# Four accumulator banks in a written order, and attention pieces spread over the key/value tile

## The chip, the cores and the metric

The kernel runs on one core of a Trainium2 chip. The metric is the device time of one execution in microseconds (us): the kernel before takes 1521.53 us, median of 3 runs (1521.13 to 1522.24).

## The reference

One layer of a hybrid decoder in float32, width 1024: a half-step SwiGLU feed-forward, a mixer, a second half-step feed-forward, each with RMS norms before and after. 512 prompt tokens with 16 meta tokens in front, and 8 running sequences with 4 new tokens each (32 sample tokens), go through the same weights. The mixer adds a gated linear attention (4 heads) and a stick-breaking attention (16 heads of 64). The latter is the part the change touches:

```
z = einsum('bqhd,bkhd->bhqk', q, k) * scale + bias
l = where(mask, log_sigmoid(-z), 0)
r = cumsum(l, reverse) - l
a = where(mask, exp(log_sigmoid(z) + r), 0)
o = einsum('bhqk,bkhd->bqhd', a, v)
```

The sample tokens attend in the same way over 256 cached positions, read by a page table, and their own.

## The kernel before

**Tiles.** Activations lie transposed, features on partitions and the 560 tokens (512 + 16 + 32) along the free axis, in two halves of 280. A weight is used as a high part (rounded by a cast) and a low part (weight minus high part, on VectorE); three products of parts make one full product. Large products go by a Strassen-like scheme: `seven_steps` forms seven products of quarter matrices in four accumulators a, d, b, c. Its groups, of 12 matmuls each, run in the order a, d, b, d (second, here d2), c, a, c; the second d group uses the quarter pair "b2", the b group uses "t", the sum of quarters. Before b's group, ScalarE copies a into b (`S.copy(b, a)`, L1059); likewise b into c. Copies such as "e5" (L1049) read d away.

**Attention pairs.** The heads go in eight pairs. In the steady part a pair is a query tile (8 steps on TensorE, `Pair.queries`, one product with two accumulators, one for each token half) and a key/value tile (14 steps, `values_keys`, by `seven_steps`). While the tiles of one pair run, the pieces of the attention of the pair before are dealt out: `scores` (a head's scores in three PSUM banks, two sigmoids on each bank, L1997 "keep" and L1998 "beta", causal masks on GpSimd, L2002), `scan` (running products on VectorE, L2011, in four pieces of 144, 272, 400 and 528 columns), `weigh` (one product of 1343 columns and two copies, L168 and L2022), `rows_v` and `rows_k` (transposes and outputs), `tails`, `turned` (transposes of the weights, L2073). The query tile ends in `queries`: ScalarE writes the high part (L1914), VectorE the residual (L171) and sample columns (L1923), both reading the query accumulators.

**Order.** Within the mixer the order of TensorE, VectorE, ScalarE and GpSimd is the order in which the program issues: a table of steps says behind which step of the tile a piece is issued (`pieces` in the list that `then` fills, and `weights_at` for the casts and low parts of the weight quarters b1, t, b2, t4). Each engine executes its own list in order, so an instruction that waits holds all behind it. SyncE issues most transfers in order; GpSimd issues the accumulating ones (L644, L649), which add a second weight block onto one that SyncE has loaded (L640, L641, L648).

**Banks.** Accumulators come from a pool of four PSUM buffers under one tag. A buffer is chosen when an accumulator is first written in program order: the one that has been free longest. In the key/value tile, a is written first, then b (by the copy, in issue order), then d, and d gets the buffer of the query tile's first half, last read by L171.

**Rooms.** SBUF is cut into rooms. Which one each `take` gets is written in a table, `PLACES`, made for one order of the program. Two uses of a room must not overlap, so a new user waits for the last reader.

**Samples.** From the fifth pair on, transposes of cached keys (`sample_keys`, L2176, at steps SK) and products with them (`sample_products`, L2190, at steps SP) are dealt in too; the pages are asked for a pair ahead (L2128).

Of the kernel before, what the change touches and what calls it, by code (L numbers as in the profile page):

```python
# [16 lines left out]
P = 128  # L17
# [36 lines left out]
1824065c540c372a763c3e20808c6e5292844e4a507a82727c62787464608e0288408670324c121e66947e583b2e10466844420122348a901400  # L54
5a126c30486a3f171456582a38003a040c8e3654026460147486324c5c401e94707e68884319106622268a34906a2428480842066c30844a9278
7a8c62520c2e5080402a6e1d1c7d181a084e825c5a3f100c120a7c207214461d092a2e42085c447d1a3f6e061b130c0f2b7c5a0a182c107d4647
5c086f1944410f16135e6e2c2a180c5a7c3f6f1a460d5d195b16410e121518142e446e2a7c6f5a0c1c1a410d5c15141146126e2c186f2a2b1c5a
7d0e0c4115145c467c0e2e6e6f7d2a2c1918415c1c145d6b7a7c0e100c746e62643284683a8e382a7888701876045224008c4836902e608a1c42
5c867e9270065e401a2a1218451d426a2e2c765a343f1c182d762a772f182b2c3f1b1c2a762f1b1c2e2b2c2d2a485a122a0626081b453a648c38
7072762924868a900c6e362e88000e04623f0a341c3230084e06418e7c6c281b60822484261e01733937110d687402922c2a422e21718d3b9189  # L60
6f6605878b65506a945453447851460f18585621807e41666019767c1a22508e6c6a1e525118202125416a84261e7468501842922e822c282a24
067a203f145a124a5e160a5c4c884172646e86056a034870398a903a92930c2e008c37113625822c026422527a3f343a5a501c140d7224869041
68200518848a926a2e261e6e6f9332742a302539061a03640a8c6872824c205c2c22528604127a368418904a5e320c378a1143426a2e39912888
25000418021a1c41172484924e8c682a707212506e30647a6f143f1634624a0c078a0d060a0811483c906874883e5e281e5f2a5a6a8c70422236
382c2e5052647a8272620c866e342549203c122c2a3a365c1e1f2e5a144a4c2f4812082a383406251f0a3c2a48122f5a32304a1e23165e215c06
3b08391f362c340a3c125a3625485e3032123b4d2a085c062c162e4a0a5e213428363c262b485a5e30321e2a25061428224d080a123c163f5c26
5e3634082b48123c5b363a483230381e4d4b2508285e260a16065c14224a383a5a482e2a08123c06374822341e2e2c2030363f2508483d4c4a3c
5a345c285f2620131e2a08155a373f251f060a322e2c0812303c3834363a481e3d4a15135f4c3208382a1e300a3c5a2512203806322c222b2e1e
0a4c085c5e364a3034483215063c083e22365a1234280232152026124a142a18406252309284242c50383a281e0a624c2e481032170008223e16
50483c200626405228141e343000241402062c9284402e62164c08521e223e160a3e0026244c002862480a20503c4c062c481614002e50183f52  # L70
1416081e0a4a222b12202a3d062d0a0800023c17411a4e2e1e1c16143f2a18040252223c2e1e414e080a2a002c20161206181c003e1a403c521e
2212142e5c842f3a324f16623834925a4e09362928245c07305e842e2a284f5b244c2c22485c201e28244e93925e5a295051245c849204504b48
4e294f240c5a648e46944282807c90726a8a667a707476887e446c55608c00683461380a32366f023c783a184f4e406216861b04143e126e1d1c
614e504a525854559248768e4d091b06023c7818601b843b7430643a60003236348d680a380b391b8c886e60446c687e6d8d557170668b8a6780
# [62 lines left out]
def hybrid_step(  # L137
# [17 lines left out]

    def whole(n):

        r = [take(3 * NT) for _ in range(-(-n // 3))]
        return [r[i // 3][:, NT * (i % 3) : NT * (i % 3) + NT] for i in range(n)], r

    count = [0]

    def ps(tag="ps"):
        count[0] += 1
        return pp.tile([P, 512], F32, tag=tag, name=f"{tag}{count[0]}")

    def tt(out, a, b, op, eng=None):
# [2614 lines left out]
```

## Time and profile before

| | |
|---|---|
| median of the runs | 1521.53 us |
| the profiled execution | 1521.29 us |
| its span | 1519.6 us |
| TensorE busy | 1486.7 us, 98% |
| VectorE busy | 1103.6 us, 73% |
| ScalarE busy | 820.7 us, 54% |
| GpSimd busy | 81.3 us, 5% |

The profiled execution lies inside the range of the timed runs; 1.7 us of it lie outside the span. The eight attention pairs take the stretch from about 570 to 830 us. Rows of the chip's timeline read: start, duration, engine, line, operation, output and input tiles, shape, count, and in brackets the idle time before it with what ended it. A row with "x4" covers four instructions from the first start to the last end.

### The profile page before, as it was taken

What the parts mean: (1) busy time and instruction counts of PE and PEld (TensorE: products, weight loads), DVE (VectorE), ACT (ScalarE), POOL (GpSimd) and SP (SyncE); (2) the same over time, 40 slices, a digit from 0 to 9 for tenths busy, and PEclk for the clock granted to TensorE, in tenths of its full rate; (3) what the DMA queues carried; (4) which work ended last, traced back from release to release, by engine and by line L of the source; (5) the groups of instructions that cost most, each with busy time, mean ns of one, the idle gap of its engine ahead of it and who ended that gap; (6) DMA issues with size and microseconds to landing.
All of it is one profiled execution on the core that took longest, in us unless ns stands there. A gap on an engine that the chain in (4) does not pass through costs nothing.

```text
span 1519.6 us, 29801 instructions
## 1 busy us (share of the span) xinstructions
PE 1486.7 (98%) x11825; PEld 1435.8 (94%) x11825; DVE 1103.6 (73%) x1860; ACT 820.7 (54%) x1537; POOL 81.3 (5%) x175
## 2 busy tenths in 40 slices
PE   9999999999999999899889999999999999999998
PEld 8999999999999888888778999999999999999998
DVE  5888888944677767777767745666567998888554
ACT  6545454633655647667665644644564554455434
POOL 2000000000000121112211000000000000000000
PEclk9999999999999999999999999999999999999999
DMA  8123333334673795556665766534632333332253
GB/s 248 56 84 99 97 98 98 89 99 142 163 155 108 177 167 134 99 112 117 136 94 148 218 162 215 114 97 107 180 109 80 93 99 98 111 98 86 86 153 113
DMA packets 288541, 187.61 MB, mean 123 GB/s; under 512 B 10988, under 2 KB 266674, under 8 KB 288402
## 3 DMA queue, kind: packets, MB, share of 16 engines
q1 hardware_dynamic: 280706, 181.97, 45.2%
q0 software_dynamic: 7680, 3.74, 2.5%
q8 instruction: 93, 1.52, 0.4%
q14 instruction: 46, 0.38, 0.1%
q10 hardware_dynamic: 16, 0.00, 0.0%
HBM read 160.63 MB, written 25.03 MB: 122 GB/s over the span
## 4 chain that ended last, share of the span: by engine, by line
PE 91%; DVE 4%; ACT 2%; issue 1%; DMA 1%; SPq 1%; DVEq 0%; ACTq 0%
PE acc L1291 8%; PE acc L1290 7%; PE acc L1289 7%; PE acc L732 6%; PE acc L733 6%; PE acc L735 6%; PE acc L719 5%; PE acc L720 4%; PE acc L722 4%; PE acc L1069 4%; PE acc L1071 4%; PE acc L1070 4%; PE acc L1232 2%; PE acc L1229 2%; PE acc L1230 2%; DVE room L168 1%
## 5 line engine op out<-in xcount | busy, mean ns | idle before, releaser
L168 DVE TENSOR_TENSOR room<-room,room 128x560 fp32r<-128x560 f32 (+17 forms) x451 | 290.4, 664 | 82.5 <-ACT room L799 18.3
L168 DVE TENSOR_TENSOR lo<-raw,hi 128x1024 fp32r<-128x1024 f32 (+1 forms) x207 | 248.0, 1199 | 95.7 <-ACT hi L697 48.4
L1291 PE MATMUL acc<-room,lo 128*128 128x280 f32 (+1 forms) x896 | 260.0, 290 | 0.0
L1290 PE MATMUL acc<-room,hi 128*128 128x280 f32 (+1 forms) x896 | 259.6, 290 | 0.0
L1289 PE MATMUL acc<-room,hi 128*128 128x280 f32 (+1 forms) x896 | 259.5, 290 | 0.0
L997 ACT CAST hi<-raw 128x1024 fp32r<-128x1024 f32 x114 | 120.1, 1057 | 142.7 <-PE acc L1290 49.3
L719 PE MATMUL acc<-room,hi 128*128 128x280 f32 x608 | 174.8, 304 | 0.2 <-DVE room L171 0.2
L1069 PE MATMUL acc<-room,hi 128*128 128x280 f32 x476 | 149.0, 313 | 23.8 <-DVE room L171 22.8
L1291 PEld LDWEIGHTS acc<-room,lo 128*128 128x128 f32 x896 | 168.8, 188 | 0.0
L1289 PEld LDWEIGHTS acc<-room,hi 128*128 128x128 f32 x896 | 168.7, 188 | 0.0
L1290 PEld LDWEIGHTS acc<-room,hi 128*128 128x128 f32 x896 | 168.5, 188 | 0.0
L720 PE MATMUL acc<-room,hi 128*128 128x280 f32 x608 | 163.9, 289 | 0.0
L1071 PE MATMUL acc<-room,lo 128*128 128x280 f32 (+1 forms) x476 | 141.4, 297 | 0.1
L1070 PE MATMUL acc<-room,hi 128*128 128x280 f32 (+1 forms) x476 | 141.0, 296 | 0.0
L697 ACT CAST hi<-raw 128x1024 fp32r<-128x1024 f32 (+1 forms) x93 | 93.6, 1006 | 76.2 <-issue 22.7
L997 ACT CAST hi<-room 128x1024 fp32r<-128x1024 f32 x106 | 89.4, 843 | 82.0 <-PE acc L1290 59.9
L168 DVE TENSOR_TENSOR lo<-room,hi 128x1024 fp32r<-128x1024 f32 x106 | 101.2, 955 | 44.0 <-ACT hi L997 43.8
L722 PE MATMUL acc<-room,lo 128*128 128x280 f32 x608 | 126.1, 289 | 0.0
L719 PEld LDWEIGHTS acc<-room,hi 128*128 128x128 f32 x608 | 114.4, 188 | 7.7 <-issue 5.6
L1069 PEld LDWEIGHTS acc<-room,hi 128*128 128x128 f32 x476 | 92.5, 194 | 30.4 <-issue 28.6
L720 PEld LDWEIGHTS acc<-room,hi 128*128 128x128 f32 x608 | 114.6, 189 | 0.9
L732 PE MATMUL acc<-room,hi 128*128 128x280 f32 (+2 forms) x388 | 110.7, 295 | 0.0
(405 smaller groups left out, 3654.0 us busy)
## 6 DMA issues: line engine op xcount, KB each, us to landing
raw<-in_w_in_dram SPq DMA_DIRECT2D x68, 256.0 KB, 5.1
raw<-in_ffn_w_gate_dram SPq DMA_DIRECT2D x64, 256.0 KB, 3.2
raw<-in_ffn_w_up_dram SPq DMA_DIRECT2D x64, 256.0 KB, 3.4
raw<-in_ffn_w_down_dram SPq DMA_DIRECT2D x36, 448.0 KB, 3.7
raw<-in_w_in_dram SPq DMA_DIRECT2D x29, 512.0 KB, 7.3
out_dram<-room SPq DMA_DIRECT2D x36, 256.0 KB, 5.4
room<-in_cache_k_dram SPq DMA_DIRECT2D x32, 256.0 KB, 5.5
room<-in_cache_v_dram SPq DMA_DIRECT2D x32, 256.0 KB, 5.8
```

Source lines behind the costliest of these rows:

```text
L168: (eng or V).tensor_tensor(out=out, in0=a, in1=b, op=op)
L719: T.matmul(acc[h][:, :w], hi[k], act.get(k, h, w)[0], start=(k == order[0]), stop=False, skip_group_check=True)
L720: T.matmul(acc[h][:, : wid[h]], hi[k], a[h][1], start=False, stop=False, skip_group_check=True)
L722: T.matmul(acc[h][:, : wid[h]], lo[k], a[h][0], start=False, stop=(k == order[-1]), skip_group_check=True)
L732: T.matmul(acc[h][:nw, : wid[h]], wh, a[h][0], start=(k == 0), stop=False)
L997: S.copy(hi[:, :kt], src)
L1069: T.matmul(x[:, :n], hi, act_[k][0][:, :n], start=(first and k == 0), stop=False, skip_group_check=True)
L1070: T.matmul(x[:, :w], hi, act_[k][1][:, :w], start=False, stop=False, skip_group_check=True)
L1071: T.matmul(x[:, :w], lo, act_[k][0][:, :w], start=False, stop=(k == 3), skip_group_check=True)
L1289: T.matmul(x[:, :QW], hi, act[k][0], start=(first and k == 0), stop=False, skip_group_check=True)
L1290: T.matmul(x[:, :QW], hi, act[k][1], start=False, stop=False, skip_group_check=True)
L1291: T.matmul(x[:, :QW], lo, act[k][0], start=False, stop=(k == 3), skip_group_check=True)
```

## The change

Four things are rewritten.

- **Banks.** The accumulators have four buffers of one tag each (acc0 to acc3), taken in a written rotation; `seven_steps` and the feed-forward's seven products each permute the rotation for those that follow. In the key/value tile of a plain pair d now takes the buffer that c had a pair earlier, last read by a ScalarE copy; b takes that of query half 0, c that of query half 1.
- **Scores by bank.** `scores` is called for one bank at a time, at steps 2, 3, 5 for the first head and 7, 10, 12 for the second, instead of all three at steps 2 and 4.
- **Pieces.** Scans, weightings, key rows and tails follow: the first weighting at step 9 instead of 7, the second at 14 instead of 12; key rows at 11 instead of 8. Steps 1 to 8 are the query tile, 9 to 22 the key/value tile. In the weight parts, t is cast one step sooner, b2 two steps later, t4 one. Sample keys, sample products and the page loads move too.
- **Rooms.** `PLACES` is a new table for the new order.

```diff
-1824065c540c372a763c3e20808c6e5292844e4a507a82727c62787464608e0288408670324c121e66947e583b2e10466844420122348a901400
+1824062b1f3c5a12107a7792469472788c90324c6a888286487e8e3a68804a0284406c7c643655448a30622f1666607050524e0c3874426e560c
...
+    pa = ctx.enter_context(tc.tile_pool(name="pa", bufs=1, space=bass.MemoryType.PSUM))
...
-    count = [0]
+    count, banks = [0], [0, 1, 2, 3]
 
     def ps(tag="ps"):
         count[0] += 1
+        if tag == "acc":
+            banks.append(banks.pop(0))
+            return pa.tile([P, 512], F32, tag=f"acc{banks[-1]}", name=f"acc{count[0]}")
         return pp.tile([P, 512], F32, tag=tag, name=f"{tag}{count[0]}")
...
-    def weights_at(when, n, f, sums=(-10, -10, -9, -8), b1=(-6, -5)):
+    def weights_at(when, n, f, sums=(-10, -10, -9, -8), b1=(-6, -5), t=(-2, -1), b2=(0, 1), t4=(4, 6)):
...
-        for key, d, e in (("b1", *b1), ("t", -2, -1), ("b2", 0, 1), ("t4", 4, 6)):
+        for key, d, e in (("b1", *b1), ("t", *t), ("b2", *b2), ("t4", *t4)):
...
         a, d, b, c = (ps("acc") for _ in range(4))
+        banks[:] = [banks[i] for i in (2, 1, 0, 3)]
...
             a, d, b, c = (ps("acc") for _ in range(4))
+            banks[:] = [banks[i] for i in (2, 0, 1, 3)]
...
-        def scores(self, e):
+        def scores(self, e, n):
...
-            for n, what in enumerate(BANKS):
...
+            if n == 0:
+                self.wide[e] = take(NW_), take(NW_)
+            beta, keep = self.wide[e]
+            at = (0, 416, 832)[n]
+            p = ps()
+            c = 0
+            for i, k0, k1 in BANKS[n]:
...
-            if e:
+            if e and n == 2:
                 give(*qs, *ks)
...
-    SK, SP, TURN = (7, 9, 11, 12), (11, 14), (15, 16, 17, 18, 19, 20)
+    SK, SP, TURN = (4, 7, 13, 14), (9, 16), (15, 16, 17, 18, 19, 20)
...
-                weights_at(then, BEGIN[pr] + TILE, ("kv", pr), (-6, -6, -5, -4))
+                weights_at(then, BEGIN[pr] + TILE, ("kv", pr), (-6, -6, -5, -4), t=(-3, -2), b2=(2, 3), t4=(5, 7))
...
-            pieces = [(2, now.scores, 0), (3, now.scan, 0, 0), (3, now.scan, 0, 1), (3, now.meta), (4, now.scores, 1), (4, now.scan, 0, 2),
-                      (5, now.scan, 0, 3), (6, now.rows_v), (7, now.weigh, 0), (8, now.rows_k), (9, now.scan, 1, 0), (9, now.scan, 1, 1),
-                      (10, now.scan, 1, 2), (10, now.tails), (11, now.scan, 1, 3), (12, now.weigh, 1)]
+            pieces = [(2, now.scores, 0, 0), (3, now.scores, 0, 1), (3, now.meta), (3, now.scan, 0, 0), (3, now.scan, 0, 1), (5, now.scores, 0, 2),
+                      (5, now.scan, 0, 2), (6, now.scan, 0, 3), (6, now.rows_v), (7, now.scores, 1, 0), (8, now.scan, 1, 0), (9, now.scan, 1, 1),
+                      (9, now.weigh, 0), (10, now.scores, 1, 1), (11, now.scan, 1, 2), (12, now.scores, 1, 2), (12, now.tails),
+                      (13, now.scan, 1, 3), (14, now.weigh, 1)]
+            pieces.insert(-3, (11, now.rows_k))
...
-                then(BEGIN[pr] + 13, lambda b=pr - 4: kps.update(pages_of(ck, 0, b)))
+                then(BEGIN[pr] + 15, lambda b=pr - 4: kps.update(pages_of(ck, 0, b)))
```

In the changed kernel line numbers are 4 to 7 higher: L168 becomes L172, L171 L175, L1923 L1929, L1049 L1054, L1059 L1064, L1069 to L1071 become L1074 to L1076, L1914 L1920, L1997 L2002, L1998 L2003, L2002 (the mask) L2007, L2011 L2016, L2022 L2027, L2073 L2078, L2176 L2181, L2190 L2195, L644 and L649 become L648 and L653.

First place: VectorE from the second half of the query tile of the fourth pair to the low part of b2. `acc582` and `acc583` are the accumulators of the two query halves, `raw` a loaded weight, "128x1343" a weighting. Before:

```order
L168 TENSOR_TENSOR room54_120_7307<-room54_120_7307,room60_10_110 128x1343
L2022 COPY room78_68_4576<-room54_120_7307 128x6x16 x2
L168 TENSOR_TENSOR lo594_7833<-room18_64_4257,hi594_7832 128x1024
L171 SCALAR_TENSOR_TENSOR room48_119_7004<-acc582_7709,room48_119_7004 64x280 x2
L171 SCALAR_TENSOR_TENSOR room48_119_7004<-acc583_7710,room48_119_7004 64x232 x2
L1923 TENSOR_SCALAR room24_1_66<-acc583_7710 64x4x4 x4
L2011 SCALAR_TENSOR_TENSOR room72_62_4255<-room72_62_4255,room78_68_4576 128x144
L2011 SCALAR_TENSOR_TENSOR room72_62_4255<-room72_62_4255,room78_68_4576 128x272
L168 TENSOR_TENSOR lo596_7859<-raw570_7547,hi596_7858 128x1024
```

With the change:

```order
L172 TENSOR_TENSOR lo590_7810<-room90_132_7140,hi590_7809 128x1024
L2016 SCALAR_TENSOR_TENSOR room90_132_7140<-room90_132_7140,room84_35_273 128x144
L175 SCALAR_TENSOR_TENSOR room42_131_7019<-acc582_7723,room42_131_7019 64x280 x2
L175 SCALAR_TENSOR_TENSOR room42_131_7019<-acc583_7724,room42_131_7019 64x232 x2
L1929 TENSOR_SCALAR room78_49_871<-acc583_7724 64x4x4 x4
L2016 SCALAR_TENSOR_TENSOR room90_132_7140<-room90_132_7140,room84_35_273 128x272
L172 TENSOR_TENSOR room72_110_5559<-room72_110_5559,room18_77_4588 128x1343
L2027 COPY room66_71_4267<-room72_110_5559 128x6x16 x2
L2016 SCALAR_TENSOR_TENSOR room90_132_7140<-room90_132_7140,room84_35_273 128x400
L172 TENSOR_TENSOR lo598_7903<-raw569_7571,hi598_7902 128x1024
```

The weighting and a scan of 400 columns have moved from ahead of the query residual to between it and the low part of b2.

Second place: ScalarE in the same stretch, from the cast of t ("hi594", now "hi590") to the copy of a into b. Before:

```order
L997 CAST hi594_7832<-room18_64_4257 128x1024
L2030 COPY room90_63_4256<-ps595_7851 128x512
L997 CAST hi596_7858<-raw570_7547 128x1024
L1914 ACTIVATE room48_119_7004<-acc582_7709 64x280 x2
L1914 ACTIVATE room48_119_7004<-acc583_7710 64x232 x2
L1059 COPY acc599_7875<-acc597_7873 128x280
```

With the change:

```order
L1001 CAST hi590_7809<-room90_132_7140 128x1024
L2046 COPY room48_75_4586<-ps591_7819 128x512
L2002 ACTIVATE room90_132_7140<-ps592_7833,sbb_101 128x416
L2003 ACTIVATE room30_94_5268<-ps592_7833,sbb_101 128x416
L1920 ACTIVATE room42_131_7019<-acc582_7723 64x280 x2
L1920 ACTIVATE room42_131_7019<-acc583_7724 64x232 x2
L1064 COPY acc595_7863<-acc593_7861 128x280
```

The cast of b2 and the key copy no longer stand ahead of the query copies; two sigmoids of the second head do, and the first of them writes room 90, which held t and which the low part of t reads.

Third place: GpSimd in the third and fourth pair. L2002 (now L2007) are causal masks, four a head. Before:

```order
L644 DMA raw558_7437<-in_w_in_dram 128x4x128
L2002 AFFINE_SELECT room54_120_7307<-room54_120_7307 128x128 x4
L649 DMA room18_64_4257<-in_w_in_dram 128x4x128
L2002 AFFINE_SELECT room54_120_7307<-room54_120_7307 128x128 x4
L644 DMA raw589_7776<-in_w_in_dram 128x4x128
```

With the change:

```order
L648 DMA raw557_7446<-in_w_in_dram 128x4x128
L2007 AFFINE_SELECT room18_77_4588<-room18_77_4588 128x128
L2007 AFFINE_SELECT room72_110_5559<-room72_110_5559 128x128 x3
L653 DMA room90_132_7140<-in_w_in_dram 128x4x128
L2007 AFFINE_SELECT room72_110_5559<-room72_110_5559 128x128 x4
L648 DMA raw588_7784<-in_w_in_dram 128x4x128
L2007 AFFINE_SELECT room72_110_5559<-room72_110_5559 128x128
```

Each accumulating transfer now stands ahead of the last mask of a head.

More of the change, by code (lines that the diff above doesn't have):

```diff
@@ L58 @@
[L58 to L62, printed above, removed]
@@ new lines, in scores @@
+            if n == 0:
[5 more added lines that the diff above has]
+            for i, k0, k1 in BANKS[n]:
+                qc, kc = slice(P * i, P * i + P), slice(k0, k1)
+                o = p[:, c : c + k1 - k0]
+                T.matmul(o, qs[e][:, qc], ks[e][:, kc], start=True, stop=False)
+                T.matmul(o, qs[e][:, qc], kl[e][:, kc], start=False, stop=True)
+                c += k1 - k0
@@ new lines, in scores @@
+            d = slice(at, at + c)
+            S.activation(keep[:, d], p[:, :c], AF.Sigmoid, bias=sbb[:, 16 + hh : 17 + hh], scale=-1.0)
+            S.activation(beta[:, d], p[:, :c], AF.Sigmoid, bias=sbb[:, hh : hh + 1])
+            for i, a, b in PARTS:
+                if (0, 0, 1, 2)[i] == n:
+                    d = beta[:, b - P : b]
+                    G.affine_select(out=d, in_=d, pattern=[[-1, P]], compare_op=ALU.is_ge, fill=0.0, base=-1,
+                                    channel_multiplier=1)
```

66 lines of the change are left out of this document (26 added, 40 removed).

## The prediction

> **What bounds the kernel now.** I read the page first, then PE's waits, then the busy time by stage, then the timeline of one pair.
>
> ```profile
> PE 1486.7 (98%) x11825; PEld 1435.8 (94%) x11825; DVE 1103.6 (73%) x1860; ACT 820.7 (54%) x1537; POOL 81.3 (5%) x175
> ...
> PE acc L1069 <- DVE room L171: 22.8, 7, 4.4
> ...
> PE acc L1069 <- ACT room L2452: 0.8, 1, 0.8
> ...
> 625.00:655.00 30.00, 26.38 (x190) 24.23 (x189) 22.77 (x47) 17.83 (x35) 7.44 (x15) 0.94 0.49 97
> ...
> 1075.00:1500.00 425.00, 425.00 (x3380) 424.42 (x3379) 317.52 (x490) 211.24 (x355) 0.00 (x0) 1.00 0.36 105
> ```
>
> TensorE is the bound, and in the last feed-forward stage it is never idle (425.00 of 425.00 us): a new rotation of banks can win nothing there. What can be won lies in the attention pairs: seven waits, one in each key/value tile, 22.8 us, for the query residual (L171). The window 625 to 655 us, one pair, also shows less than the full clock (0.94).
>
> ```profile
> 599.69 0.37 PE L1069 MATMUL acc<-room,hi 128*128 128x280 f32 x1 [2.52 <-DVE room L171]
> 631.34 0.37 PE L1069 MATMUL acc<-room,hi 128*128 128x280 f32 x1 [3.62 <-DVE room L171]
> 663.52 0.57 PE L1069 MATMUL acc<-room,hi 128*128 128x280 f32 x1 [2.69 <-DVE room L171]
> 694.28 0.57 PE L1069 MATMUL acc<-room,hi 128*128 128x280 f32 x1 [2.68 <-DVE room L171]
> ...
> 697.21 0.29 PE L1069 MATMUL acc<-room,hi 128*128 128x280 f32 x1
> ...
> 698.76 0.29 PE L1069 MATMUL acc<-room,hi 128*128 128x280 f32 x1
> ...
> 725.94 0.37 PE L1069 MATMUL acc<-room,hi 128*128 128x280 f32 x1 [2.64 <-DVE room L171]
> 760.18 0.57 PE L1069 MATMUL acc<-room,hi 128*128 128x280 f32 x1 [4.22 <-DVE room L171]
> 797.02 0.57 PE L1069 MATMUL acc<-room,hi 128*128 128x280 f32 x1 [4.41 <-DVE room L171]
> ```
>
> After the wait at 694.28 the twelve matmuls of group d take 2.93 us (to 697.21), the twelve of b after them 1.55 us: a slowed clock costs another 1.3 us, in five tiles of seven (not behind 2.52 and 2.64). The waits so cost about 22.8 + 5 x 1.3 = 29.3 us; with the small one 30.1 us.
>
> **The change part by part.** I follow the fourth pair, whose query tile starts (Q) at 676.87.
>
> ```profile
> 676.87 0.29 PE L719 MATMUL acc<-room,hi 128*128 128x280 f32 x1
> ...
> 689.49 0.38 PE L1069 MATMUL acc<-room,hi 128*128 128x280 f32 x1
> ...
> 691.11 0.27 PE L2048 MATMUL ps<-ident,room 128*48 128x128 f32 x1
> ...
> 691.33 0.27 PE L2050 MATMUL ps<-ident,room 128*96 128x128 f32 x1
> ...
> 707.68 0.29 PE L719 MATMUL acc<-room,hi 128*128 128x280 f32 x1
> ```
>
> *Banks.* Group d was given the bank of query half 0 and waited for L171. Now d takes a bank that ScalarE emptied long ago, and that half's bank goes to b, written first by the copy L1059 (now L1064), one group later. That removes the wait on L171 if L171 is done by then.
>
> *Pieces on TensorE.* They only change place: two score banks and the key transposes (four matmuls each, together about 1.4 us) leave the query tile for the key/value tile, all before the group d2, the fourth, which uses b2. So d2 is due where it would be now without the wait: 12.62 (689.49 - 676.87) + a 1.62 + tails 0.33 + d 1.55 + b 1.55 = Q+17.7; its first low part (third matmul) is due at Q+17.9. From d2's start to the next query tile are 8.9 us (698.76 to 707.68).
>
> *VectorE.* This chain decides.
>
> ```profile
> 682.57 1.07 DVE L2011 TENSOR_TENSOR_SCAN room<-room,room 128x144 f32<-128x144 f32 x2 [3.15 <-ACT room L1997]
> ...
> 686.15 1.23 DVE L168 TENSOR_TENSOR lo<-raw,hi 128x1024 fp32r<-128x1024 f32 x1 [1.40 <-ACT hi L997]
> 687.30 0.98 DVE L2011 TENSOR_TENSOR_SCAN room<-room,room 128x400 f32<-128x400 f32 x1
> 688.20 0.67 DVE L168 TENSOR_TENSOR room<-raw,room 128x512 f32<-128x512 f32 x1
> 688.78 1.25 DVE L2011 TENSOR_TENSOR_SCAN room<-room,room 128x528 f32<-128x528 f32 x1
> 690.14 1.56 DVE L168 TENSOR_TENSOR room<-room,room 128x1343 f32<-128x1343 f32 x1
> ...
> 691.98 1.22 DVE L168 TENSOR_TENSOR lo<-room,hi 128x1024 fp32r<-128x1024 f32 x1
> 693.22 1.75 DVE L171 SCALAR_TENSOR_TENSOR room<-acc,room 64x280 fp32r<-64x280 f32 x4
> 694.99 0.53 DVE L1923 TENSOR_SCALAR room<-acc 64x16 f32<-64x16 f32 x4
> 695.54 1.25 DVE L2011 TENSOR_TENSOR_SCAN room<-room,room 128x144 f32<-128x144 f32 x2
> 696.72 1.24 DVE L168 TENSOR_TENSOR lo<-raw,hi 128x1024 fp32r<-128x1024 f32 x1
> ```
>
> Steps below are distances from one start to the next. The first scan starts at Q+5.7 (682.57) in both kernels: the same score bank and sigmoid release it. Then come two scans 1.0, two weight sums 2 x 0.6, the low part of b1 1.15, scans 0.9 and 1.36, the low part of t 1.24: Q+12.5. The idle 1.40 before b1 goes, since its cast now stands ahead of most sigmoids.
>
> The first sigmoids of the second head are written into the room that the low part of t has just read. ScalarE so waits until Q+12.5; four query copies are queued behind.
>
> ```profile
> 685.98 0.66 ACT L1997 ACTIVATE room<-ps,sbb 128x416 f32<-128x416 f32 x1
> 686.48 0.65 ACT L1998 ACTIVATE room<-ps,sbb 128x416 f32<-128x416 f32 x1
> ...
> 691.92 1.60 ACT L1914 ACTIVATE room<-acc 64x280 fp32r<-64x280 f32 x4
> ```
>
> Two sigmoids (0.5 each) and the first copy (0.4) put L175, once L171, at Q+13.9, against Q+16.35 (693.22); where only the second sigmoid meets that room, at Q+13.4. The two of half 0 end 0.9 us later, and the copy for b (taken at 0.4, like a query copy) is done by about Q+15.2; b is due at 17.7 - 1.55 = Q+16.1: the old wait goes, with 0.9 us to spare.
>
> But the low part of b2 now stands behind the first head's weighting. L175 1.8, L1929 0.55, a scan 0.6, weighting and copies 1.84, scan 0.9, b2 1.2: 6.9 us, so it is ready at Q+20.8 (20.3 in the other case). Today it is ready at Q+21.1 (696.72 + 1.24), which is early enough only because TensorE has waited. **The stall moves to d2**, 2.9 us (2.4): this is the price I take. Its lower bound is 0, if the order of VectorE runs 2.9 us sooner; its upper bound 4.4, the longest wait seen at this place.
>
> Three of the four plain tiles have 2.9, one 2.4: 11.1 us. Whether the clock drops, the rows leave at the edge (2.64 and 2.52 no, 2.68 yes); I count it in two of them, 2.6 us. [...]
>
> In the last three tiles sample keys take part. Four sets of transposes (0.6 us each, less where the next work overlaps them) and half the products (0.3) stand ahead of d2 on TensorE: about 2 us, which VectorE's chain does not have. I take a wait of 1.0 us for each tile, 3.0 in all, bounds 0 and 2.9, with no slow clock.
>
> ```profile
> 726.78 0.60 PE L2176 MATMUL ps<-ident,room 128*128 128x128 f32 x4
> 727.31 0.64 PE L2190 MATMUL ps<-room,room 128*32 128x256 f32 x8
> ...
> 756.86 0.58 ACT L2030 COPY room<-ps 128x512 f32<-128x512 f32 x1 [2.19 <-DVE lo L168]
> ```
>
> That is where most is gained: there the key copy (756.86) waited 2.19 us for a room, queued ahead of the query copies; it now stands behind them.
>
> *GpSimd and the queues.* The accumulating load for the next tile now stands between the causal masks of the second head, and it waits for a load that SyncE issues only after the first weighting (Q+18.4).
>
> ```profile
> 661.00 0.37 SPq L648 DMA_DIRECT2D room<-in_w_in_dram  x1
> 687.84 0.50 SPq L641 DMA_DIRECT2D raw<-in_w_in_dram  x1
> 665.49 1.29 POOL L649 DMA_DIRECT2D room<-in_w_in_dram  x1 [0.67 <-DMA room<-in_w_in_dram]
> 694.61 1.28 POOL L644 DMA_DIRECT2D raw<-in_w_in_dram  x1 [9.07 <-DVE room L171]
> ```
>
> With 4.5 us for that load (661.00 to 665.49) and about 1.1 for its issue and the last mask, the second weighting starts at Q+24 instead of 23.2, and the second head's transposes wait some 0.5 us (0 to 0.8): 3.5 us over seven tiles. The page loads are asked two steps later and used three sooner, eleven steps (some 15 us) ahead: I cost them at nothing.
>
> *Sum.* 30.1 go; 11.1 + 2.6 + 3.0 + 3.5 = 20.2 come. 9.9 us are gained on the profiled execution's 1521.3, which lies within 0.3 us of the median: **1511 us**.
>
> **The rivals.**
> 1. *The wait goes altogether*: b2 arrives by Q+17.9. For it: VectorE is busy only 22.77 of 30 us. Against it: 6.9 us are queued between L175 and b2. 1521.3 - 29.3 = 1492 us; 0.17.
> 2. *Nothing is won*: every tile waits 2.9 and drops the clock, 7 x 4.2 = 29.4: within 0.2% of 1521; 0.10. So too if d still met the query's bank.
> 3. *Slower*: the first weighting waits for the first head's last mask, which now stands behind GpSimd's accumulating load L644, itself waiting for L641. That took 6.8 us from issue to start (687.84 to 694.61). Issued at about Q+9.0 now, it frees the mask at Q+16.9 (1.1 us on), and the weighting is due at Q+16.8: the cover is nil to 2 us. Each microsecond more delays b2 in seven tiles; from 1.9 us on the 9.9 and another 3 are gone. At 2.2 us with four more slowed clocks: 1511 + 15.4 + 5.2 = 1532 us; 0.15.
>
> **How the numbers follow.** Forecast 0.58, rivals 0.17, 0.10 and 0.15. About 0.2% (3 us) is what can be told from no change: faster 0.75, same 0.10, slower 0.15. The forecast's own range is 1500 to 1517. To leave out no more than 2 in 10, the range reaches towards the first rival, whose full gain needs every wait gone, and over the second: 1496 to 1523.
>
> **What would show it.** PE's waits should name the low part (L172) at d2's third matmul, L1076, in the plain tiles, 2.4 to 2.9 us; the line L175 should be gone from them. In VectorE's timeline L175 should start 13.4 to 13.9 us after the query tile, and b2's low part end at 20.3 to 20.8. If L1064 is named, L175 is later than I think; if transposes (L2078) are, GpSimd's masks are; if sample transposes (L2181) are, pages are late. No wait above 0.5 us in the tiles would make the first rival right.

## The result, and the profile after

The changed kernel takes 1513.84 us (median of four runs, 1511.87 to 1517.31), the kernel before beside it 1521.88 us. The ratio is 0.9948, with an interval of 0.9927 to 0.9968: faster by 8.0 us, where 1511 us and a gain of about 10 were forecast. Timed once more beside the kernel before (the run x9 below), the ratio was 0.9957 (0.9943 to 0.9972), a gain of 6.1 us.

The profiled execution is the slowest of the four, 1517.31 us, with a span of 1515.6. TensorE's waits in that execution, with the time in total, how often, and the longest; the small ones, which stood in the kernel before too, are left out.

```profile
PE acc L1076 <- DVE lo L172: 7.4, 3, 2.9
PE ps L2078 <- DVE room L172: 5.1, 3, 2.6
PE ps L2160 <- POOL room L2148: 3.4, 1, 3.4
PE acc L1074 <- ACT room L1054: 1.9, 3, 0.9
```

The wait of 22.8 us on the query residual is gone from the key/value tiles, and four others stand in its place, 17.8 us together. In the timeline of TensorE they fall mostly in the four plain tiles:

```profile
600.54 0.39 PE L1074 MATMUL acc<-room,hi 128*128 128x280 f32 x1 [0.75 <-ACT room L1054]
603.34 0.40 PE L1076 MATMUL acc<-room,lo 128*128 128x280 f32 x1 [2.27 <-DVE lo L172]
...
638.38 0.24 PE L2160 MATMUL ps<-ident,room 32*128 32x32 f32 x1 [3.40 <-POOL room L2148]
...
670.35 0.40 PE L1074 MATMUL acc<-room,hi 128*128 128x280 f32 x1 [0.32 <-ACT room L1054]
673.14 0.60 PE L1076 MATMUL acc<-room,lo 128*128 128x280 f32 x1 [2.27 <-DVE lo L172]
...
702.01 0.40 PE L1074 MATMUL acc<-room,hi 128*128 128x280 f32 x1 [0.88 <-ACT room L1054]
705.39 0.60 PE L1076 MATMUL acc<-room,lo 128*128 128x280 f32 x1 [2.85 <-DVE lo L172]
```

Three plain tiles show a pair of waits at d2: a short one until ScalarE has copied d away (L1054), and two matmuls later the one for b2's low part. The second plain tile, at 638.38, has none of the two; there TensorE waits for a mask of the sample tokens. The windows over the seven tiles (length, busy time of PE, weight loads, VectorE, ScalarE and GpSimd, then granted clock, DMA share and GB/s) show that the clock did not recover in the plain pairs, those of the first four key/value tiles:

```profile
590.00:625.00 35.00, 29.34 (x199) 27.02 (x198) 23.24 (x44) 20.21 (x39) 7.21 (x10) 0.90 0.44 92
625.00:655.00 30.00, 26.60 (x182) 24.92 (x182) 23.43 (x47) 18.61 (x37) 10.06 (x14) 0.89 0.49 96
655.00:685.00 30.00, 27.41 (x200) 25.79 (x196) 23.17 (x42) 21.13 (x40) 7.65 (x10) 0.94 0.48 97
685.00:720.00 35.00, 31.27 (x220) 28.31 (x217) 25.65 (x48) 21.14 (x40) 7.19 (x10) 0.90 0.75 133
...
755.00:790.00 35.00, 34.21 (x263) 30.38 (x262) 28.10 (x50) 26.26 (x50) 8.08 (x13) 1.00 0.63 129
790.00:825.00 35.00, 34.88 (x276) 30.91 (x274) 27.36 (x49) 26.77 (x52) 5.40 (x11) 1.00 0.69 127
```

In the window 590 to 625 us the clock is 0.90, where the kernel before had 1.00, and from 625 to 655 us 0.89 against 0.94. The last two windows, with sample tiles, are at full clock and nearly without idle time (34.21 and 34.88 of 35.00 us): it is there that the gain is made. The start of each pair's query tile (the first matmul of L719, now L723), in us from the start of the execution, shows how much:

| query tile of pair | 2 | 3 | 4 | 5 | 6 | 7 | 8 |
|---|---|---|---|---|---|---|---|
| before | 613.00 | 646.09 | 676.87 | 707.68 | 740.34 | 776.97 | 814.16 |
| change | 617.96 | 652.22 | 683.35 | 716.50 | 749.15 | 780.80 | 811.65 |
| change, again (x9) | 618.19 | 650.88 | 681.55 | 714.65 | 747.25 | 778.95 | 809.81 |

The plain pairs lose: at the fifth pair the change is 8.8 us late (7.0 in x9). The sixth and seventh pairs win 11.3 us, so that the eighth starts 2.5 us early (4.4 in x9).

The chain on VectorE in the fourth pair, the one that the prediction followed; its query tile starts at 683.35:

```profile
697.74 1.75 DVE L175 SCALAR_TENSOR_TENSOR room<-acc,room 64x280 fp32r<-64x280 f32 x4 [0.73 <-ACT room L1920]
...
701.23 1.63 DVE L172 TENSOR_TENSOR room<-room,room 128x1343 f32<-128x1343 f32 x1 [0.42 <-POOL room L2007]
...
704.14 1.19 DVE L172 TENSOR_TENSOR lo<-raw,hi 128x1024 fp32r<-128x1024 f32 x1
...
709.64 1.56 DVE L172 TENSOR_TENSOR room<-room,room 128x1343 f32<-128x1343 f32 x1 [1.98 <-POOL room L2007]
```

The residual starts 14.4 us after the query tile (697.74 - 683.35), b2's low part ends at 22.0 (704.14 + 1.19 - 683.35), and the second weighting starts at 26.3; both weightings are held by a mask of GpSimd. In the third pair (query tile at 652.22) the three are earliest, at 13.9, 20.9 and 24.5 us; in the second they are at 14.4, 21.3 and 25.4.

### The profile page after: what moved, and what is told of

It is laid out like the page before. It is cut to its first block, busy times and chain, and to the rows that moved or that the text cites. A ratio compares the mean times of both kernels' runs of the same rounds, so it can differ in the third digit from the quotient of the medians.

```text
span 1515.6 us, 29815 instructions
## 1 busy us (share of the span) xinstructions
PE 1488.7 (98%) x11825; PEld 1436.4 (95%) x11825; DVE 1100.7 (73%) x1860; ACT 821.0 (54%) x1537; POOL 89.3 (6%) x175
## 4 chain that ended last, share of the span: by engine, by line
PE 91%; DVE 4%; DMA 1%; ACT 1%; issue 1%; POOL 1%; SPq 1%; DVEq 0%; POOLq 0%; ACTq 0%
PE acc L1295 8%; PE acc L1297 8%; PE acc L1296 7%; PE acc L736 6%; PE acc L737 6%; PE acc L739 6%; PE acc L723 5%; PE acc L724 4%; PE acc L726 4%; PE acc L1074 4%; PE acc L1076 4%; PE acc L1075 4%; PE acc L1237 2%; PE acc L1234 2%; PE acc L1235 2%; DVE room L172 1%
## 5 line engine op out<-in xcount | busy, mean ns | idle before, releaser
L172 DVE TENSOR_TENSOR room<-room,room 128x544 f32<-128x544 f32 (+16 forms) x439 | 285.6, 669 | 98.5 <-ACT room L803 18.0
L172 DVE TENSOR_TENSOR lo<-raw,hi 128x1024 fp32r<-128x1024 f32 (+1 forms) x207 | 248.3, 1200 | 82.4 <-ACT hi L701 44.3
L723 PE MATMUL acc<-room,hi 128*128 128x280 f32 x608 | 175.7, 306 | 0.2 <-DVE room L175 0.2
L1295 PEld LDWEIGHTS acc<-room,hi 128*128 128x128 f32 x896 | 168.8, 188 | 0.0
L1296 PEld LDWEIGHTS acc<-room,hi 128*128 128x128 f32 x896 | 168.8, 188 | 0.0
L1074 PE MATMUL acc<-room,hi 128*128 128x280 f32 x476 | 150.1, 315 | 2.2 <-ACT room L1054 1.9
L1076 PE MATMUL acc<-room,lo 128*128 128x280 f32 (+1 forms) x476 | 141.8, 298 | 7.4 <-DVE lo L172 7.4
L172 DVE TENSOR_TENSOR lo<-room,hi 128x1024 fp32r<-128x1024 f32 x106 | 100.9, 952 | 43.3 <-ACT hi L1001 43.1
L723 PEld LDWEIGHTS acc<-room,hi 128*128 128x128 f32 x608 | 114.5, 188 | 7.3 <-issue 5.6
L724 PEld LDWEIGHTS acc<-room,hi 128*128 128x128 f32 x608 | 114.6, 189 | 0.6
L736 PE MATMUL acc<-room,hi 128*128 128x280 f32 (+2 forms) x388 | 110.7, 295 | 0.0
L737 PE MATMUL acc<-room,hi 128*128 128x280 f32 (+2 forms) x388 | 108.8, 290 | 0.0
```

Source lines behind the costliest of these rows:

```text
L172: (eng or V).tensor_tensor(out=out, in0=a, in1=b, op=op)
L723: T.matmul(acc[h][:, :w], hi[k], act.get(k, h, w)[0], start=(k == order[0]), stop=False, skip_group_check=True)
L724: T.matmul(acc[h][:, : wid[h]], hi[k], a[h][1], start=False, stop=False, skip_group_check=True)
L736: T.matmul(acc[h][:nw, : wid[h]], wh, a[h][0], start=(k == 0), stop=False)
L737: T.matmul(acc[h][:nw, : wid[h]], wh, a[h][1], start=False, stop=False)
L1074: T.matmul(x[:, :n], hi, act_[k][0][:, :n], start=(first and k == 0), stop=False, skip_group_check=True)
```

## The experiments

All of them compute the whole reference. Each row has the medians of the kernel and of the kernel before beside it, and the ratio with its interval.

| run | what it is | us | before | ratio |
|---|---|---|---|---|
| x1 | the new order without the banks | 1518.34 | 1522.98 | 0.9971 (0.9961 to 0.9981) |
| x2 | the banks in the old order | 1516.23 | 1522.98 | 0.9954 (0.9937 to 0.9970) |
| x3 | b2's low part ahead of the first weighting | 1541.74 | 1522.98 | 1.0134 (1.0117 to 1.0151) |
| x4 | a new order of the pieces | 1492.92 | 1522.98 | 0.9804 (0.9787 to 0.9820) |
| x5 | x3, accumulating loads three steps later | 1500.66 | 1522.45 | 0.9852 (0.9835 to 0.9868) |
| x6 | the change, accumulating loads three steps later | 1506.33 | 1522.45 | 0.9891 (0.9872 to 0.9909) |
| x7 | x4, sample rows six steps later | 1488.09 | 1522.45 | 0.9773 (0.9757 to 0.9789) |
| x8 | x4 without the banks | 1492.11 | 1522.45 | 0.9798 (0.9782 to 0.9815) |
| x9 | the change once more | 1515.50 | 1521.61 | 0.9957 (0.9943 to 0.9972) |
| x10 | the banks in the old order once more | 1514.95 | 1521.61 | 0.9951 (0.9938 to 0.9965) |

### The two halves of the change apart

The run x1 is the changed kernel with its accumulators back in the common pool:

```diff
-    pa = ctx.enter_context(tc.tile_pool(name="pa", bufs=1, space=bass.MemoryType.PSUM))
...
-        if tag == "acc":
-            banks.append(banks.pop(0))
-            return pa.tile([P, 512], F32, tag=f"acc{banks[-1]}", name=f"acc{count[0]}")
```

> The changed kernel without its written rotation of banks: the four accumulators come from the common pool again. Theory A (the order of the pieces makes the gain, the banks only say where TensorE waits): d gets query half 0's buffer again and waits for L175, whose first two end about 14.8 us after the query tile's start, while d is due at 13.2: about 1.5 us in each plain tile, and b2's low part then delays d2 by only about 1 us more, so each pair ends where it did. Time 1512 to 1518 us, waits for L175 in most tiles, none above 2 us. Rival B (the banks make the gain): 1520 us or more, waits for L175 as long as before the change.

The run x2 is the kernel before with those lines, the list of banks and its two permutations added; the rooms, scores, pieces and weight parts stay as they were.

> The kernel before with the written rotation of banks alone, order and rooms untouched. Theory A: the wait on L171 moves from d to b, one group later; b's copy is ready at about 17.6 us after the query tile's start and b due at 16.1, so about 1.5 us, and b2's low part (ready at 21.1) holds d2 for another 1.7 us. Each pair ends about 1.0 us sooner, and since no wait is above 2.5 us some of the five slow stretches (1.3 us each) go too: 1506 to 1514 us. Rival B (the banks alone are the change's gain): the same range, so the waits tell: B has the waits on L171 gone. Rival C (a stall moved is a stall kept): 1519 to 1522 us.

Measured were 1518.34 us, just above the range expected, and 1516.23 us, 2 us above it. The waits of TensorE in x1:

```profile
PE ps L2074 <- DVE room L168: 10.4, 5, 4.1
PE acc L1070 <- DVE room L171: 7.7, 4, 2.1
PE acc L1072 <- DVE lo L168: 4.4, 3, 2.1
```

With the pool the wait on the residual (L171 here too) is back, though only in the four plain tiles and with 2.1 us at most instead of 4.4, since the residual now comes earlier. These three waits sum to 22.5 us, as much as the 22.8 of the kernel before, yet the run is 4.6 us faster. Its stretch from 590 to 830 us has a granted clock of 0.99, against 0.95 before (the profiled execution is the fastest of its nine). In x2:

```profile
PE acc L1074 <- ACT acc L1064: 7.1, 5, 2.5
PE ps L2196 <- ACT room L2184: 6.0, 3, 2.4
PE acc L1076 <- DVE lo L172: 3.6, 3, 1.3
```

With the banks alone, b waits in the plain tiles for the copy of a (L1064), which must not write the query half's bank before the residual has read it. In the sample tiles the products wait for a copy of ScalarE. So the banks by themselves take the wait off d; what remains is shorter than before (16.7 us in these three). The waits on b and d2 came about as expected; those of the products, 6.0 us, were in no step of the expectation.

Because the two medians, 1513.84 of the change and 1516.23 of x2, lay too close to tell, both were timed side by side, as x9 and x10.

> The change itself again, beside x10 on one chip, to tell what its order of pieces adds to its banks. Theory A (the order's own new stalls, b2's low part and the masks, give back what it wins, so it adds under 4 us to the banks): 1511 to 1515 us, ratio to the kernel before 0.993 to 0.996. Rival B (the order adds 5 us or more): under 1511 us.

> The kernel before with the banks alone again (as x2), beside x9. Theory A: 1514 to 1517 us, ratio 0.9945 to 0.9965, less than 4 us above x9. Rival B: 5 us or more above x9.

They came out at 1515.50 (0.9943 to 0.9972), half a microsecond above the range expected, and 1514.95 us (0.9938 to 0.9965), inside it: no difference beyond some 2 us, which is what six runs of each can tell. So the banks alone gain as much as the whole change, and the order alone gains 4.6 us: the two do not add up. They win in different ways. With the order alone the query tiles of the fifth and eighth pairs start at 714.77 and 810.32 us, 7.1 us late and 3.8 early, as with the change; with the banks alone at 708.77 and 811.16, 1.1 us late and 3.0 early. The order wins some 11 us in the sample tiles and gives most of it back in the plain ones; the banks win less and lose little.

### Where the new wait comes from

The prediction held that b2's low part is late because the first head's weighting stands ahead of it. The run x3 puts it ahead (the new table of rooms that every such order needs is left out here and below):

```diff
-            when(n + e, parted_lo, f, key, key in ("b1", "b2"))
+            when(n + e, parted_lo, f, key, key == "b1" or key == "b2" and d != 1)
+            if key == "b2" and d == 1:
+                when(n + 3, st.fetch)
...
-                weights_at(then, BEGIN[pr] + TILE, ("kv", pr), (-6, -6, -5, -4), t=(-3, -2), b2=(2, 3), t4=(5, 7))
+                weights_at(then, BEGIN[pr] + TILE, ("kv", pr), (-6, -6, -5, -4), t=(-3, -2), b2=(1, 1), t4=(5, 7))
...
-                      (9, now.weigh, 0), (10, now.scores, 1, 1), (11, now.scan, 1, 2), (12, now.scores, 1, 2), (12, now.tails),
+                      (10, now.weigh, 0), (10, now.scores, 1, 1), (11, now.scan, 1, 2), (12, now.scores, 1, 2), (12, now.tails),
```

> The changed kernel with b2's cast one and its low part two steps sooner and the first weighting one step later, so that the low part of b2 stands ahead of the weighting on VectorE; the load that the low part set off is still issued at step 11. Theory A (the new stall is b2's low part, queued behind the weighting): the low part is ready at about 18.1 us after the query tile's start instead of 20.8, the waits at d2's third matmul (2.3 to 2.9 us) fall below 0.5, the first transposes of the weights then wait about 1.4 us for the weighting; 1504 to 1510 us. Rival B (d2 is held by the copy of d on ScalarE or by the load): d2 still waits over 2 us, 1512 to 1516 us.

Measured: 1541.74 us, 1.3% slower than the kernel before. The mechanism was right and the time wrong. The waits of TensorE in x3:

```profile
PE ps L2080 <- DVE room L172: 37.8, 9, 9.7
PE ps L2162 <- POOL room L2150: 2.7, 1, 2.7
PE acc L1076 <- ACT acc L1066: 1.3, 4, 0.4
```

No wait for a low part is left at d2. Instead the transposes of the second head (L2080) wait up to 9.7 us each for the weighting. The timeline of SyncE's queue, ScalarE, GpSimd and VectorE in one tile says why:

```profile
708.85 0.47 SPq L644 DMA_DIRECT2D raw<-in_w_in_dram  x1
...
709.04 0.73 ACT L2005 ACTIVATE room<-ps,sbb 128x512 f32<-128x512 f32 x1
709.37 1.02 SPq L645 DMA_DIRECT2D raw<-in_w_in_dram  x1
...
710.67 0.42 SPq L652 DMA_DIRECT2D room<-in_w_in_dram  x1
...
720.74 1.29 POOL L653 DMA_DIRECT2D room<-in_w_in_dram  x1 [9.70 <-DMA room<-in_w_in_dram]
721.52 0.82 POOL L2009 TENSOR_SCALAR_AFFINE_SELECT room<-room 128x128 f32<-128x128 f32 x1
722.38 1.56 DVE L172 TENSOR_TENSOR room<-room,room 128x1343 f32<-128x1343 f32 x1 [8.05 <-POOL room L2009]
```

GpSimd's accumulating load L653 adds onto what L652 loads, and so it waits for that (9.70 us in its row) and starts 10.1 us after the issue of L652. The second head's last mask stands behind L653; the sigmoid that it masks (L2005) had ended at 709.8 us. The weighting waits for the mask, and TensorE for the weighting. In the same pair of the changed kernel L652 is issued at 702.89 us and L653 starts at 708.00, 5.1 us later. What differs in x3 is that two other loads, L644 and L645, are issued just ahead of L652 and not behind it. That they are why it took 10 us was not tried by itself; in the second and third pairs of x3, with the same two loads ahead, L652 landed 5.3 and 5.1 us after its issue.

If that reading holds, a later accumulating load must mend x3, and help the change by what its transposes and its sample mask wait. In x5 and x6 the accumulating loads of the steady part are issued three steps later, behind all masks of the head; x5 has this on top of x3, x6 on top of the change:

```diff
-                        nc.gpsimd.dma_start(raw[:, 4:], x, accum_op=ALU.add)
+                        added(lambda: nc.gpsimd.dma_start(raw[:, 4:], x, accum_op=ALU.add))
...
-                        nc.gpsimd.dma_start(t3, w[0][: 4 * P, c0 : c0 + nw].rearrange("(k p) n -> p k n", p=P), accum_op=ALU.add)
+                        y3 = w[0][: 4 * P, c0 : c0 + nw].rearrange("(k p) n -> p k n", p=P)
+                        added(lambda: nc.gpsimd.dma_start(t3, y3, accum_op=ALU.add))
...
+    adds = [0]
+
+    def added(f):
+        later(adds[0], f) if adds[0] else f()
...
+            adds[0] = 3 if 25 < n < BEGIN[8] - 14 else 0
```

> The order of x3 (b2's low part ahead of the first weighting), with each accumulating load of GpSimd issued three steps later in its list, behind the masks it stood before. Theory A (x3 is slow because the second head's last mask stands behind an accumulating load that waits for its own first load, up to 9.7 us): the second head's transposes wait under 1.5 us instead of 3.4 to 9.7, d2 stays free, the first head's transposes wait about 1 us: 1500 to 1508 us. Rival B (VectorE is too late there anyway): above 1520 us.

> The changed kernel with nothing else than the accumulating loads issued three steps later, behind the masks. Theory A: the waits of transposes (5.1 us in three tiles) fall below 1.5, the waits of d2 for b2's low part (2.3 to 2.9 us) stay as they are: 1508 to 1512 us. Rival B (the pair ends where b2 and the next query tile let it): 1513 to 1516 us.

Measured: x5 1500.66 us, as expected and 41 us under x3, and x6 1506.33 us, a little below what was expected, 7.5 us under the change's first median and 9.2 under its second. The waits of x6:

```profile
PE acc L1082 <- DVE lo L172: 7.0, 3, 2.5
PE ps L2166 <- POOL room L2154: 2.3, 1, 2.3
PE acc L1080 <- ACT room L1060: 2.1, 3, 0.9
```

The transposes' wait is gone, the sample mask's is 1.1 us shorter, and d2's stays. In x5, which puts b2 ahead as well, d2's is gone too. So both reasons are real: b2's low part stands too late on VectorE, and the accumulating load too early on GpSimd.

### An order that has neither

The run x4 joins both remedies, and moves the second head's scores behind the query copies, so that the copies on ScalarE no longer stand behind sigmoids that wait for t's room:

```diff
-            pieces = [..., (7, now.scores, 1, 0), (8, now.scan, 1, 0), (9, now.scan, 1, 1),
-                      (9, now.weigh, 0), (10, now.scores, 1, 1), (11, now.scan, 1, 2), (12, now.scores, 1, 2), (12, now.tails),
-                      (13, now.scan, 1, 3), (14, now.weigh, 1)]
-            pieces.insert(-3, (11, now.rows_k))
+            pieces = [..., (10, now.weigh, 0), (10, now.scores, 1, 0), (11, now.scan, 1, 0),
+                      (11, now.scores, 1, 1), (12, now.scan, 1, 1), (12, now.rows_k), (12, now.scores, 1, 2), (13, now.scan, 1, 2), (13, now.tails),
+                      (14, now.scan, 1, 3), (15, now.weigh, 1)]
...
-    SK, SP, TURN = (4, 7, 13, 14), (9, 16), (15, 16, 17, 18, 19, 20)
+    SK, SP, TURN = (4, 7, 13, 14), (9, 16), (16, 17, 18, 20, 21, 22)
```

The last pair keeps its old steps for the transposes; b2 and the accumulating loads stand as in x5.

> The changed kernel with the second head's scores put behind the query copies (steps 10 to 12), b2's low part ahead of the first weighting (step 10), scans at 11 to 14, the second weighting at 15, the second head's transposes at 20 to 22, and the accumulating loads issued three steps later, behind the masks. Theory A (VectorE's order and ScalarE's room wait cost all that is left): L175 starts at about 12.5 us after the query tile's start, b2's low part ends at 16.0, the weighting at 17.9, the second at 24.0; no wait above 0.7 us in the plain tiles; 1494 to 1502 us. Rival B (VectorE is itself full): b2 and the weightings still arrive late, 1506 us or more.

> The order of x4 without the written rotation of banks, accumulators from the common pool as before. Theory A (the banks only decide who waits when the query residual is late): with L175's first two done 0.5 us before d is due, nothing waits for them, 1492 to 1495 us. Rival B (the banks carry part of the gain in any order): 1497 us or more, with waits on L175.

Measured: 1492.92 us, a little below the range expected, and without the banks 1492.11 us. The residual starts 12.6 to 13.0 us after the query tile in the plain pairs and b2's low part ends at 16.2 to 16.6, near the 12.5 and 16.0 expected. What the move of the scores does apart from the other edits of x4 was not timed. In this order the banks make no difference, though the residual is named again without them (3.2 us in four tiles, 1.1 at most). In x4 TensorE's largest waits are

```profile
PE ps L2168 <- POOL room L2156: 2.6, 1, 2.6
PE ps L2086 <- DVE room L172: 1.9, 3, 0.7
```

The first of them is the sample mask of the second plain tile, which the change has too (L2160, 3.40 us). GpSimd's timeline of the changed kernel, in that tile, shows it behind the accumulating load, as the last of four masks (first and last shown):

```profile
631.91 1.27 POOL L648 DMA_DIRECT2D raw<-in_w_in_dram  x1 [5.17 <-PE ps L1999]
...
634.22 0.40 POOL L2146 TENSOR_SCALAR_AFFINE_SELECT room<-room 32x64 f32<-32x64 f32 x1
...
637.19 1.14 POOL L2148 TENSOR_SCALAR_AFFINE_SELECT room<-room 32x64 f32<-32x64 f32 x1
```

The masks are issued by `sample_rows`, a piece dealt out once, at step 8 of that pair; the transposes that read them belong to `sample_rows_out`, dealt out at step 13. The run x7 deals out the latter six steps later:

```diff
-        then(BEGIN[2] + 13, sample_rows_out)
+        then(BEGIN[2] + 19, sample_rows_out)
```

> The order of x4 with the one piece that still waited, the transposes of the sample masks, moved from step 13 to 19 of its pair. Theory A: that wait of 2.58 us and the slow stretch behind it (1.3 us) go: 1488.5 to 1490.5 us. Rival B (the wait is caught up later in the pair): 1492 to 1493.5 us.

Measured: 1488.09 us (1487.67 to 1489.54), just under the range expected and the fastest of all kernels here, 2.3% under the kernel before. The stretch from 590 to 830 us runs at full clock with TensorE busy for 237.68 of 240 us, so little is left to win there:

```profile
590.00:830.00 240.00, 237.68 (x1951) 216.80 (x1950) 205.78 (x386) 178.07 (x343) 59.71 (x91) 1.00 0.68 140
```

### Waits and clock together

In this table the waits are TensorE's in the profiled execution that are not the same in every kernel, summed from 0.2 us up. The slowed matmuls are those of L1074 to L1076 and L723 to L727 (and the same lines of the other kernels) between 590 and 830 us whose row is 0.42 us long or longer; each costs about 0.1 us more than at the fast pace (0.23 us from start to start instead of 0.13).

| kernel | waits, us | slowed matmuls | span, us |
|---|---|---|---|
| before | 25.7 | 57 | 1519.6 |
| change | 19.3 | 60 | 1515.6 |
| change, again (x9) | 22.3 | 30 | 1513.8 |
| order alone (x1) | 24.8 | 15 | 1515.3 |
| banks alone (x2) | 20.9 | 40 | 1515.9 |
| x6 | 12.2 | 42 | 1505.3 |
| x4 | 5.9 | 20 | 1491.9 |
| x7 | 3.0 | 0 | 1486.3 |

For the change, waits and matmuls give a gain of 6.4 - 3 x 0.1 = 6.1 us, and 4.0 are in the span; for x9 3.4 + 2.7 = 6.1 against 5.8, for x1 0.9 + 4.2 = 5.1 against 4.3, for x2 4.8 + 1.7 = 6.5 against 3.7. So the sum is good to 1 us or to 3. In its profiled execution x1 gains by the clock (15 slowed matmuls instead of 57), and hardly by waiting less (24.8 us instead of 25.7). For x4 and x7 the sum is 4.2 and 4.9 us short of the span; the transposes that are slowed in the same stretches are not counted, and how much of the rest they make was not worked out.

## Why the prediction was right, and where it was off

**The bound and the place: right.** TensorE's waits in the key/value tiles set the time, and the last feed-forward stage gained nothing: it was without idle time before, and is so after (404.97 of 405.00 us from 1075 to 1480). Most was to be gained in the sample tiles, and was.

**The banks: right, and more than they were credited with.** The wait on the residual went. The prediction tied this to the new order, which brings the residual forward to 13.9 us. x2 and x10 show that the order was not needed for the gain: with the old order the banks leave b a wait of 1.35 to 2.5 us on its copy in the plain tiles, and win as much. x1 shows the reverse: without the banks the order wins 4.6 us, and the pairs start much as with them.

**The plain tiles: wrong as a whole.** By the prediction's terms they come out even: 11.5 us of waits and three slowed stretches of 1.3 go, 15.4 us; 11.1 + 2.6 and four times 0.5 for transposes come, 15.7. Measured, the fifth pair starts 8.8 us late, 7.0 in x9. The sample tiles were to win 9.4 us (13.9 less 3.0 and 1.5) and won 11.3. The total was so near partly by luck: what was priced too low in the plain tiles is in part made up by what was priced too high.

**VectorE's chain: right in its order, 0.5 to 2.3 us early.** In the fourth pair the residual was forecast at 13.9 us and came at 14.4, the end of b2's low part at 20.8 and came at 22.0, the second weighting at 24 and came at 26.3. In the third pair only the second sigmoid waits for t's room; there 13.4 and 20.3 were forecast, 13.9 and 20.9 measured. The half microsecond is in the first query copy: it starts at 696.91 us and the residual 0.83 us later, where 0.4 was taken.

**The wait at d2: right in kind, near in size.** 11.1 us were forecast in four tiles; three have it, 7.4 us for the low part and 1.9 for the copy of d away, 9.3 in all. That copy (L1054) was in no step of the prediction. In the fourth pair the low part is 1.2 us later than forecast and the wait for it still 2.85 us, since d2 itself is due later. In the second tile the sample mask came in its place, 3.4 us that the prediction did not see: it followed GpSimd's masks of the prompt only.

**The sample tiles: too dear.** 1.0 us each was taken; the measured wait at d2 there is none. The price stood between 0 and 2.9 without a row for it, and the lower bound was right.

**The transposes: 3.5 us forecast over seven tiles, 5.1 measured in three** (2.63, 1.75 and 0.69 us). The mechanism was the named one, the last mask behind the accumulating load; x6 removes it and gains 7.5 to 9.2 us with it. In x9 the transposes wait 7.5 us.

**The clock: the term that was most mis-sized.** Two slowed stretches, 2.6 us, were to come back. Five did in the profiled execution, some 6 us of matmuls, and three in the execution of x9. This term (some 3.4 us in the first profile), the sample mask (3.4) and the transposes (1.6) came out dearer than the forecast, the sample tiles (3.0) and the wait at d2 (1.8) cheaper: 3.6 us on balance, where 1.9 to 3.8 us of the forecast gain were missing (8.0 and 6.1 measured).

**The rivals.** That all waits go (1492 us) was not so here; x4 shows that it takes another order, and its time came out there, 1492.92, with 5.9 us of waits left, so that the agreement is in part chance. That nothing is won is excluded by both intervals. The slower case did not occur in the change, though its mechanism did, by 0.42 us in the fourth pair (0.85 in x9): the first weighting waits for the first head's last mask. The 6.8 us that the prediction read for L641 are not that load's alone, since the row names VectorE's residual as what ended the wait. The same mechanism, a mask held behind an accumulating load that waits for a load of SyncE, is what made x3 19 us slower than the kernel before; there it struck the second head and L652, not the first head and L641, as the prediction had it.

**Page loads at nothing: right.** No wait of TensorE names them.

## What to carry to other kernels

Here a rotation of buffers moved a wait to the next accumulator (7.1 us on b in x2); before crediting one, follow the waiting engine's queue to the operand that is due next, and price that. Look at what stands behind an accumulating transfer that waits: here one of 9.70 us on GpSimd held a mask, and with it VectorE's weighting for 8.05 us (x3), and three steps of delay were worth 7.5 us or more in one order and 41 us in another. Before two edits are credited together, time each alone: here either had most of the gain, the two did not add up, and in a better order the banks made no measurable difference. Where a total comes out as forecast, look at the stages: here a loss in four pairs and a larger gain in two others stood behind a gain of 0.5%.

## What the runs showed of the hardware

A wait of nearly the same length in the same kernel was followed by slowed matmuls in one execution and not in another. In the third pair of the changed kernel, in the first profile, the matmuls after 2.27 us of waiting start 0.23 us apart:

```profile
673.54 0.43 PE L1074 MATMUL acc<-room,hi 128*128 128x280 f32 x1
673.78 0.43 PE L1075 MATMUL acc<-room,hi 128*128 128x280 f32 x1
```

In the execution of x9, after 2.18 us, they start 0.13 us apart:

```profile
671.72 0.40 PE L1076 MATMUL acc<-room,lo 128*128 128x280 f32 x1 [2.18 <-DVE lo L172]
671.96 0.29 PE L1074 MATMUL acc<-room,hi 128*128 128x280 f32 x1
672.09 0.30 PE L1075 MATMUL acc<-room,hi 128*128 128x280 f32 x1
```

In the first plain pair both executions wait 2.27 us; the first is slowed from 604.93 us on, the other is not. The granted clock of the four windows above is 0.95, 0.94, 1.00 and 0.95 in x9, against 0.90, 0.89, 0.94 and 0.90. By length alone the waits do not sort: 3.41 us in x3 (ended at 798.63 us) was not followed by slowed matmuls, and 2.10 us in x1 (ended at 633.43) was. In the record of the granted clock of the kernel before and of the change, every slowed stretch in the pairs has a clock of 0.50 and is 3.41 us long or twice that (6.83), and within one execution their starts lie whole multiples of 3.41 us apart: in the change they are at 604.86, 611.69, 639.00, 673.13 and 703.85 us, distances of 2, 8, 10 and 9 times 3.41. Cut into windows on that grid, the third pair reads as follows, first the change (busy time of TensorE, then clock), then x9:

```profile
669.72:673.13 3.41, 0.83 (x5) 1.00 0.96 186
673.13:676.54 3.41, 3.40 (x15) 0.50 0.55 156
```

```profile
666.94:670.35 3.41, 2.27 (x16) 1.00 0.88 137
670.35:673.76 3.41, 2.04 (x16) 1.00 0.46 127
```

In the first the waits of TensorE fall into one window, 2.58 us of them, and the next runs at half clock. In the other the border of two windows, at 670.35, cuts them into 0.81 and 1.37 us, and the clock stays. In the traces of the kernel before and of the change (waits over 0.15 us counted, between 590 and 830 us) no window at full clock with 1.75 us of waits or less in it was followed by a slowed one, and each with 1.89 us or more was. That the border of the windows is the cause was not tried by a run. Where the clock fell, a wait cost more than its length: in the kernel before, the twelve matmuls behind the wait that ended at 694.28 us took 2.93 us, the twelve after them 1.55. In x1, where two waits are above 2.2 us (4.13 and 2.47), 15 matmuls are slowed; in the kernel before, where seven waits are (2.52 to 4.41), 57, at nearly the same sum of waits.

In x5's second plain tile a wait of only 1.18 us, then sums of single columns for 1.3 us, were followed by matmuls 0.23 us apart:

```profile
632.59 0.24 PE L2168 MATMUL ps<-ident,room 32*128 32x32 f32 x1 [1.18 <-POOL room L2156]
632.67 1.30 PE L2170 MATMUL ps<-ones,room 1*128 1x1 f32 x8
633.91 0.60 PE L1082 MATMUL acc<-room,hi 128*128 128x280 f32 x1
634.31 0.44 PE L1083 MATMUL acc<-room,hi 128*128 128x280 f32 x1
```

The window of 3.41 us in which they stand has 1.65 us of waits, and the next runs at half clock; in x3 and x6 such windows had 1.78 and 1.18 us. After the same sums and a wait of 1.26 us x8 shows no slowed matmul, and nor does x7, which has them six steps later. Whether the small matmuls had a part in x5's slowed stretch was not tried.

The same load took longer to land in x3, where L644 and L645 are issued within 2 us ahead of it on the same queue: L652 landed 9.0, 5.3, 5.1 and 9.5 us after its issue in the four plain pairs, against 7.0, 4.2, 3.9 and 4.6 in the changed kernel. That the two loads are the cause was not tried.
